# Attention scores: three products of 64 rows a head on two halves of the array, in place of two of 128 rows

## The chip, the core and the metric

One Trainium2 chip, of which one core runs the program. The metric is the device time of one execution in microseconds; the median of three runs of the kernel before is 1757.9 us (1756.42 to 1758.44).

The engines are named as the profile names them: PE is TensorE's matrix products, PEld its loads of stationary operands (weights), DVE is VectorE, ACT ScalarE, POOL GpSimd, SP the queue that issues DMAs. "f32" in a matmul row stands for float32 and for its rounded form fp32r alike.

## What is computed

Two layers: a Mamba-2 mixer, then stick-breaking attention over 16 heads of 64 features and 1024 positions. The change is in the scores of the second layer, cut here to what matters:

```
def stick_breaking_mixer(h, k, v, norm_g, w_in, q_g, w_out):
    ...
    q = rmsnorm(qg[..., :SB_WIDTH].reshape(bsz, s, SB_HEADS, SB_HEAD_DIM), q_g)
    q = (q * (1.0 / math.sqrt(SB_HEAD_DIM))).transpose(0, 2, 1, 3)
    for blk in range(s // SB_BLOCK):
        ...
        z = jnp.einsum('bhtd,bhsd->bhts', q[:, :, q0:kend], k[:, :, :kend]).astype(jnp.float32)
        ...
        log_keep = jnp.where(strict, jax.nn.log_sigmoid(-z), 0.0)
        suffix = lax.cumsum(log_keep, axis=3, reverse=True) - log_keep
        weights = jnp.where(strict, jnp.exp(jax.nn.log_sigmoid(z) + suffix), 0.0)
        outs.append(jnp.einsum('bhts,bhsd->bhtd', weights.astype(v.dtype), v[:, :, :kend]))
```

A float32 product is made of three products of rounded parts: with q = q_hi + q_lo and k = k_hi + k_lo it is q_hi k_hi + q_hi k_lo + q_lo k_hi.

## The kernel before

The first half of the span is the Mamba layer, and after it come an embedding stage, the attention (from about 924 us to 1531 us) and the output layers. Only the attention is touched.

The attention goes through eight pairs of heads (`hp`), and in each pair through four blocks of 256 positions (`p` = 3, 2, 1, 0), so 32 steps (`i`). For a block, `project` multiplies the activations with the pair's weights (L911, 24 products of 384 columns for 128 positions), `norm` scales keys and queries, and `flip` turns them with two transposes each (L1054) so that the 128 partitions hold the 64 features of head 0 and the 64 of head 1. `flip` then splits them into rounded and rest parts, and `scores` makes the products. Positions run backwards, so the scores of block `b` of 128 queries cover (8 - b) x 128 keys, in one part up to 512 columns and in two equal parts above. A pair of heads has, for each head, twelve such parts: widths 512 (three), 448 (two), 384 (three), 320 (two), 256 and 128.

How the parts lie before: `kst` holds for each head, in one column of 128 partitions, k_hi on the head's own 64 partitions and k_lo on the other 64. `qh` holds q_hi twice, on both halves, and `ql` holds q_lo on the own half and zeros on the other (zeroed once, L882). So one product over 128 rows with `qh` gives q_hi k_hi + q_hi k_lo (L1111), and one with `ql` gives q_lo k_hi (L1112). To lay this out, `flip` issues per step two ACT instructions for k_hi (L1064), four for q_hi (L1076), two DVE instructions for k_lo (L1067) and two for q_lo (L1081), each on 64 partitions.

After the scores, ACT takes the sigmoid (`s_sig`, L1119), which frees the PSUM tile `z`. DVE runs the product along the keys (`scan`, L1124), PE transposes the result (L1150, L1152), ACT and DVE split it into parts (L1158, L1163), and PE multiplies it with the values (L1171) in the accumulator `oq`.

The order of PE, ACT and DVE in the attention is made ahead of time by `Plan.order`: every step is an `op_` with an engine, an estimated duration, a rank, the ops that it comes after, and buffers (`slot`) that it takes and gives from rings of fixed size. At each point the op that can start first is put out next, ranks break ties, and the table `RANK` shifts the rank of a kind of op. The ring `z` has two tiles and `tr` three; `qh` has one.

Of the kernel before, what the change touches and what calls it, by code (L numbers as in the profile page):

```python
# [18 lines left out]
P = 128  # L19
S = 1024  # L20
# [20 lines left out]
FILL = {32: 7, 33: 6}  # L41
CHUNKS = {29: (0, 1), 30: (2, 3)}

RANK = {"project": 3, "copy_kq": -13, "sums": -16, "start": -28, "newton": -2587, "nmul": -6, "v_split": -57,
        "gate": 20, "sig": 55, "gmul": -17, "w_load": 6, "w_hi": -28, "w_lo": -45, "k_hi": 10, "k_lo": -32,
        "q_hi": -853, "q_lo": -3, "scores": -1586, "s_sig": -729, "scan": 8, "turn": -2674, "a_hi": 20,
        "a_lo": 1, "o_add": -18, "o_gate": 27, "store": -4, "r_lo": -919, "o_load": 7, "o_hi": 6, "f_load": 13,
        "f_split": -10, "fill": -19, "f_add": -1544}


def split3(nc, out, pairs):
# [18 lines left out]
class Plan:  # L70
# [789 lines left out]
def attention(k, A, rawp, hT, oTd, dbg, b2, pairs):  # L860


    tc, nc = k.tc, k.nc
    ident = k.ident
    hh, hl = hT
    mm = k.mm
    with ExitStack() as ctx:
        pp = ctx.enter_context(tc.tile_pool(name="b_pair", bufs=1, reuse_waits="tile"))
        wk = ctx.enter_context(tc.tile_pool(name="b_work", bufs=2, reuse_waits="tile"))
        sm = ctx.enter_context(tc.tile_pool(name="b_small", bufs=2, reuse_waits="tile"))  # L870
        zp = ctx.enter_context(tc.tile_pool(name="b_z", bufs=2, space=PSUM, reuse_waits="tile"))
# [6 lines left out]
        nc.gpsimd.tensor_copy(keep[:, :P], k.tri)  # L878
        zrow = keep[0:1, P:3 * P].bitcast(F32)
        kst = pp.tile([P, 2, S], F32R, name="kst")  # L880
        ql = pp.tile([P, 2, 256], F32R, name="ql")
        nc.gpsimd.memset(ql.bitcast(F32), 0.0)  # L882

        oqs = op.tile([P, 512], F32, name="oq")

        plan = Plan()
        for name, bufs in (("mm", 2), ("z", 2), ("tr", 3), ("w", 3), ("pt", 5), ("kq", 2), ("vr", 3), ("qh", 1), ("sg", 1),
                           ("of", 2), ("V", 6), ("vs", 1), ("raw", 3)):
# [11 lines left out]
        n = len(steps)  # L900
# [145 lines left out]
        def flip(i, hp, p):  # L1046
            tsl = slice(p * 256, (p + 1) * 256)
            t = {}

            def turn_(m):  # L1050
                def go():
                    t[m] = trp.tile([P, 512], F32, name="tr")[:, :256]
                    for j in range(2):
                        nc.tensor.transpose(t[m][:, j * P:(j + 1) * P], sts[hp]["kq", p][:, j, m], ident)  # L1054
                return go
            old = list(zs.get(i - 1, ()))
            ks, qs = slot("tr", 2), slot("tr", 2)
# [3 lines left out]
            qh_s = slot("qh", 2 * sum(len(parts(b)) for b in (2 * p + 1, 2 * p)))  # L1061

            def key_hi(h):
                return lambda: nc.scalar.activation(kst[own[h], h, tsl], t[0][own[h]], AF.Copy, scale=g[own[h]])  # L1064

            def key_lo(h):
                return lambda: nc.vector.scalar_tensor_tensor(  # L1067
                    kst[own[1 - h], h, tsl], t[0][own[h]], g[own[h]], kst[own[h], h, tsl].bitcast(F32),
                    op0=ALU.mult, op1=ALU.subtract)

            def query_hi(h):
                def go():
                    if h == 0:
                        tiles["qh", i] = wk.tile([P, 2, 256], F32R, name="qh", bufs=1)
                    for x in (own[h], own[1 - h]):
                        nc.scalar.copy(tiles["qh", i][x, h], t[1][own[h]])  # L1076
                return go

            def query_lo(h):
                o = own[h]  # L1080
                return lambda: nc.vector.tensor_tensor(ql[o, h], t[1][o], tiles["qh", i][o, h].bitcast(F32), op=ALU.subtract)  # L1081
            prev, pd = [], []
            for h in range(2):
                prev = [op_("k_hi", "ACT", 0.47, 10 * i + 2, key_hi(h), [fk] + prev + (old if p == 3 else []))]
                khi[i, h] = prev[0]
                pd = [op_("k_lo", "DVE", 0.49, 10 * i + 2, key_lo(h), [khi[i, h]] + pd, (), (ks,))]
                klo[i, h] = pd[0]
            for h in range(2):
                prev = [op_("q_hi", "ACT", 0.73, 10 * i + 2, query_hi(h), [fq] + prev, (qh_s,) if h == 0 else ())]
                pd = [op_("q_lo", "DVE", 0.43, 10 * i + 2, query_lo(h), prev + pd + old, (), (qs,))]  # L1090
                qlo[i, h] = pd[0]
# [6 lines left out]
        def scores(i, hp, h, b, qh_s):  # L1098
            N = (NT - b) * P
            qs = slice((b % 2) * P, (b % 2) * P + P)  # L1100
            pt_s[i, h, b] = slot("pt")
            key = ("a", hp, h, b)
            last = []
            sg = []
            for m, (ko, w) in enumerate(parts(b)):
                z_s = slot("z")

                def mul(ko=ko, w=w, m=m):
                    z = tiles["z", i, h, b, m] = zp.tile([P, 512], F32, name="z")
                    rk = kst[:, h, b * P + ko:b * P + ko + w]  # L1110
                    nc.tensor.matmul(z[:, :w], lhsT=tiles["qh", i][:, h, qs], rhs=rk, start=True, stop=False)  # L1111
                    nc.tensor.matmul(z[:, :w], lhsT=ql[:, h, qs], rhs=rk, start=False, stop=True)  # L1112
                z = op_("scores", "PE", 2 * (0.013 + w * 0.000419), 10 * i + 3, mul, [klo[i, h], qlo[i, h]] + last[:1], (z_s,), (qh_s,))
                zs.setdefault(i, []).append(z)

                def sig(ko=ko, w=w, m=m):
                    if m == 0:
                        tiles[key] = wk.tile([P, S], F32, name="pt", bufs=5)
                    nc.scalar.activation(tiles[key][:, ko:ko + w], tiles["z", i, h, b, m][:, :w], AF.Sigmoid, scale=-1.0)  # L1119
                s = op_("s_sig", "ACT", 0.19 + w * 0.00078, 10 * i + 3, sig, [z] + sg, (pt_s[i, h, b],) if m == 0 else (), (z_s,))  # L1120

                def scan(ko=ko, w=w):
                    pt = tiles[key]
                    nc.vector.tensor_tensor_scan(pt[:, ko:ko + w], pt[:, ko:ko + w], keep[:, ko:ko + w],  # L1124
                                                 pt[:, ko - 1:ko] if ko else 1.0, op0=ALU.mult, op1=ALU.max)
                sg = [s]
                last = [z, op_("scan", "DVE", 0.15 + w * 0.00208, 10 * i + 3, scan, [s] + last[1:])]
            scans[i, h, b] = last[1]

        def combine(i, hp, p):  # L1130
            lo = 2 * p
# [207 lines left out]
        for hp in range(8):  # L1339
            pair = [(4 * hp + 3 - p, p) for p in (3, 2, 1, 0)]  # L1340
            for i, p in pair:
                copies = project(i, hp, 2 * p + 1)
                if p == 1:
                    gate(i, hp, 1)
                if p == 1:
                    gate(i, hp, 0)
                copies += project(i, hp, 2 * p)
                norm(i, hp, p, (copies[0], copies[2]))
                values(i, hp, p, (copies[1], copies[3]))
            if hp + 1 < 8:  # L1350
                for q in range(4):
                    weights(hp + 1, q)
            if hp == 6:
                begun.append(op_("begin", "SPW", 0.0, 0, lambda: b2.begin(pairs), proj[6, 0][-1:]))
            for i, p in pair:
                qh_s = flip(i, hp, p)
                for h in range(2):
                    for b in (2 * p + 1, 2 * p):
                        scores(i, hp, h, b, qh_s)
                combine(i, hp, p)  # L1360
        for kk in range(KT):
            s_out(kk)
# [247 lines left out]
```

## Time and profile before

| | us |
|---|---|
| median of three runs | 1757.9 |
| the profiled execution, its own time | 1758.81 |
| span of that execution, first to last instruction | 1757.1 |
| PE busy | 1703.1 (97%) |
| PEld busy | 1450.7 (83%) |
| DVE busy | 1196.1 (68%) |
| ACT busy | 895.9 (51%) |

A matmul's record lasts longer than the time after which the next one starts, because matmuls are pipelined; what one costs on PE is read from the distance between two starts. A "busy" PE is therefore not PE at its peak. The form "128*64" of a matmul means 128 rows and 64 columns of the array; a product on 64 columns at partition 0 and one on 64 columns at partition 64 lie on different halves. In the Mamba layer L485 makes such products, alternating between the two halves, while all other products of that stretch use 128 rows and 128 columns.

### The profile page before, as it was taken

Reading aid. Unit: us, or ns where it says so; the run is one execution under the profiler, and the core shown is the slowest. Engines: PE = TensorE matmul, PEld = TensorE weight load, DVE = VectorE, ACT = ScalarE, POOL = GpSimd, SP = SyncE. Lnnn points to the kernel's source line nnn. Section 1 sums busy time; section 2 is a strip of 40 time slices with the busy share of each in tenths; the row PEclk is TensorE's granted clock in tenths of the full one; section 3 lists DMA queues with packets and bytes.
Section 4 is the critical chain, followed back from the end, with each engine's and each line's share of the span. In section 5 each row is a group of like instructions: output and inputs, shape, how many; then the busy total and the mean of one; then the engine's idle time right before and its main releaser. Section 6 shows DMA issues by size and latency. Waiting matters only on the chain.

```text
span 1757.1 us, 25573 instructions
## 1 busy us (share of the span) xinstructions
PE 1703.1 (97%) x9170; PEld 1450.7 (83%) x9170; DVE 1196.1 (68%) x2460; ACT 895.9 (51%) x1976; POOL 434.2 (25%) x452
## 2 busy tenths in 40 slices
PE   7999999999999999999999999999999999899999
PEld 6777877887887777888888999989999998778887
DVE  7678179259448846443567699999999999993232
ACT  6558339447635624222355556666575666652121
POOL 0134624524444322220001111121121214211010
PEclk9999999999999999999999999999999999899999
DMA  4222213213212365332221111111110112252100
GB/s 162 69 67 91 96 49 108 90 54 96 91 66 79 126 215 179 113 132 87 82 100 31 56 32 59 41 33 56 31 59 28 48 43 67 76 165 78 57 28 36
DMA packets 96399, 139.43 MB, mean 79 GB/s; under 512 B 18160, under 2 KB 66640, under 8 KB 96272
## 3 DMA queue, kind: packets, MB, share of 16 engines
q1 hardware_dynamic: 96272, 137.80, 24.4%
q8 instruction: 72, 1.18, 0.3%
q14 instruction: 55, 0.45, 0.1%
HBM read 108.77 MB, written 24.77 MB: 76 GB/s over the span
## 4 chain that ended last, share of the span: by engine, by line
PE 79%; DVE 13%; ACT 4%; DMA 2%; issue 2%; POOL 0%; SPq 0%; DVEq 0%; ACTq 0%
PE mm L54 38%; PE mm L911 17%; PE mm L1441 4%; PE oq L1171 3%; DVE pt L1124 3%; PE pq L54 3%; DVE v L310 2%; PE intra L485 2%; PE z L1111 2%; PE z L1112 2%; PE tr L1150 1%; PE tr L740 1%; DVE wl L1163 1%; PE inter L480 1%; PE tr L1152 1%
## 5 line engine op out<-in xcount | busy, mean ns | idle before, releaser
L54 PE MATMUL mm<-ul,wh 128*128 128x512 f32 (+1 forms) x648 | 254.0, 392 | 0.0
L54 PE MATMUL mm<-uh,wh 128*128 128x512 f32 (+1 forms) x648 | 252.4, 390 | 0.1
L54 PE MATMUL mm<-uh,wl 128*128 128x512 f32 (+1 forms) x648 | 252.4, 390 | 0.0
L1124 DVE TENSOR_TENSOR_SCAN pt<-pt,keep 128x320 f32<-128x320 f32 (+3 forms) x192 | 196.1, 1048 | 3.5 <-ACT pt L1119 1.4
L911 PE MATMUL mm<-g0h,hh 128*128 128x384 f32 x512 | 174.7, 341 | 3.6 <-ACT vr L952 1.8
L911 PE MATMUL mm<-g0l,hh 128*128 128x384 f32 x512 | 175.9, 343 | 0.0
L911 PE MATMUL mm<-g0h,hl 128*128 128x384 f32 x512 | 174.2, 340 | 0.0
L310 DVE SCALAR_TENSOR_TENSOR v<-u,convh,v 128x512 f32<-128x512 f32 x144 | 129.5, 904 | 55.1 <-ACT v L308 52.6
L997 POOL TENSOR_TENSOR vs<-vs,vr 128x256 f32<-128x256 f32 x32 | 30.5, 953 | 477.4 <-DMA vs<-vr 241.1
L54 PEld LDWEIGHTS mm<-ul,wh 128*128 128x128 f32 x648 | 121.7, 188 | 26.4 <-issue 2.3
L54 PEld LDWEIGHTS mm<-uh,wl 128*128 128x128 f32 x648 | 121.8, 188 | 25.5 <-issue 1.9
L54 PEld LDWEIGHTS mm<-uh,wh 128*128 128x128 f32 x648 | 121.7, 188 | 25.5 <-issue 1.1
L182 POOL TENSOR_TENSOR wl<-raw,wh 128x1024 fp32r<-128x1024 f32 x39 | 95.1, 2440 | 156.1 <-ACT wh L180 156.0
L1158 ACT CAST wh<-tr 128x512 fp32r<-128x512 f32 (+1 forms) x160 | 84.4, 547 | 64.2 <-PE tr L1152 59.1
L650 DVE SCALAR_TENSOR_TENSOR acc<-mm,rg,acc 128x512 f32<-128x512 f32 x64 | 47.8, 749 | 84.8 <-PE mm L54 83.2
L1119 ACT ACTIVATE pt<-z 128x320 f32<-128x320 f32 (+3 forms) x192 | 87.0, 492 | 36.4 <-PE z L1112 24.3
L1163 DVE TENSOR_TENSOR wl<-tr,wh 128x512 fp32r<-128x512 f32 (+1 forms) x160 | 96.6, 629 | 7.5 <-ACT wh L1158 6.1
L911 PEld LDWEIGHTS mm<-g0h,hh 128*128 128x128 f32 x512 | 96.5, 188 | 5.8 <-DVE GT L979 2.9
L911 PEld LDWEIGHTS mm<-g0h,hl 128*128 128x128 f32 x512 | 96.6, 189 | 0.9
L911 PEld LDWEIGHTS mm<-g0l,hh 128*128 128x128 f32 x512 | 96.5, 188 | 0.6
L723 DVE SCALAR_TENSOR_TENSOR pth<-pth,pq 128x512 f32<-128x512 f32 (+1 forms) x33 | 22.2, 672 | 108.2 <-PE pq L54 103.6
L447 ACT ACTIVATE ex<-ex,acum 128x128 f32<-128x128 f32 x256 | 86.5, 389 | 0.8
(378 smaller groups left out, 4316.6 us busy)
## 6 DMA issues: line engine op xcount, KB each, us to landing
raw<-in_w_in SPq DMA_DIRECT2D x40, 512.0 KB
ex<-acd SPq DMA_DIRECT2D x64, 256.0 KB
raw<-in_w_b SPq DMA_DIRECT2D x32, 512.0 KB
raw<-in_m_out SPq DMA_DIRECT2D x16, 512.0 KB
raw<-in_gate SPq DMA_DIRECT2D x16, 512.0 KB
graw<-gT SPq DMA_DIRECT2D x30, 256.0 KB
gT<-zs SPq DMA_DIRECT2D x28, 256.0 KB
acc<-in_x SPq DMA_DIRECT2D x8, 512.0 KB
```

What stands on the lines that cost most here:

```text
L54: nc.tensor.matmul(out, lhsT=a, rhs=b, start=(i == 0), stop=(i == n - 1))
L182: (eng or nc.gpsimd).tensor_tensor(lo, raw, hi.bitcast(F32), op=ALU.subtract)
L310: nc.vector.scalar_tensor_tensor(vv, u[:, 3 - j:3 - j + 512], w(j), vv, op0=ALU.mult, op1=ALU.add)
L447: nc.scalar.activation(x, x, AF.Relu, bias=acum[:, c:c + 1])
L650: nc.vector.scalar_tensor_tensor(acc[:, sl], ps, k.rg[:, g, t:t + 1], acc[:, sl], op0=ALU.mult, op1=ALU.add)
L911: nc.tensor.matmul(out, lhsT=a, rhs=b, start=(i == 0), stop=(i == len(prs) - 1))
L1119: nc.scalar.activation(tiles[key][:, ko:ko + w], tiles["z", i, h, b, m][:, :w], AF.Sigmoid, scale=-1.0)
L1124: nc.vector.tensor_tensor_scan(pt[:, ko:ko + w], pt[:, ko:ko + w], keep[:, ko:ko + w], pt[:, ko - 1:ko] if ko else 1.0, op0=ALU.mult, op1= ...
L1158: nc.scalar.copy(wh[:, :c], tiles["tq", key][:, :c])
L1163: nc.vector.tensor_tensor(wl[:, :c], tiles["tq", key][:, :c], wh[:, :c].bitcast(F32), op=ALU.subtract)
L1171: nc.tensor.matmul(out[:, :w], lhsT=sts[hp]["V"][j // 2][:, j % 2, h * P:(h + 1) * P], rhs=rhs, start=(j0 == lo and m == 0), stop=(j0 == N ...
L1441: nc.tensor.matmul(pss[n], lhsT=a, rhs=b, start=(q == 0 and i == 0), stop=(q == 1 and i == 11))
```

## The change

`kst` now holds k_hi of both heads in its first half and k_lo of both heads in its second, each on the head's own 64 partitions; `qh` holds q_hi and q_lo in the same way, in two buffers where there was one. `ql` and its zeros are gone. `flip` issues one instruction per step for each of k_hi, k_lo, q_hi and q_lo, on 128 partitions. A score op makes both heads at once: three products of 64 rows for each, head 0 on rows 0 to 63 of the array and head 1 on rows 64 to 127, in alternation, into two `z` tiles that it takes together. Three products are still accumulated for each score. `RANK` has new numbers, and with them the order of PE, ACT and DVE in the attention is another; of that table two lines stand here.

```diff
-RANK = {"project": 3, "copy_kq": -13, "sums": -16, "start": -28, "newton": -2587, "nmul": -6, "v_split": -57,
+RANK = {"project": 6, "copy_kq": 33, "copy_v": -1481, "square": 9, "sums": 6, "start": 11, "nmul": -17,
...
-        ql = pp.tile([P, 2, 256], F32R, name="ql")
-        nc.gpsimd.memset(ql.bitcast(F32), 0.0)
...
-            ks, qs = slot("tr", 2), slot("tr", 2)
+            ks, qs = slot("tr"), slot("tr")
...
-            def key_hi(h):
-                return lambda: nc.scalar.activation(kst[own[h], h, tsl], t[0][own[h]], AF.Copy, scale=g[own[h]])
...
-                    for x in (own[h], own[1 - h]):
-                        nc.scalar.copy(tiles["qh", i][x, h], t[1][own[h]])
...
+            def key_hi():
+                nc.scalar.activation(kst[:, 0, tsl], t[0], AF.Copy, scale=g)
+
+            def key_lo():
+                nc.vector.scalar_tensor_tensor(
+                    kst[:, 1, tsl], t[0], g, kst[:, 0, tsl].bitcast(F32), op0=ALU.mult, op1=ALU.subtract)
+
+            def query_hi():
+                tiles["qh", i] = wk.tile([P, 2, 256], F32R, name="qh", bufs=2)
+                nc.scalar.copy(tiles["qh", i][:, 0], t[1])
+
+            def query_lo():
+                q = tiles["qh", i]
+                nc.vector.tensor_tensor(q[:, 1], t[1], q[:, 0].bitcast(F32), op=ALU.subtract)
...
-                z_s = slot("z")
+                z_s = [slot("z") for _ in range(2)]
...
-                    z = tiles["z", i, h, b, m] = zp.tile([P, 512], F32, name="z")
-                    rk = kst[:, h, b * P + ko:b * P + ko + w]
-                    nc.tensor.matmul(z[:, :w], lhsT=tiles["qh", i][:, h, qs], rhs=rk, start=True, stop=False)
-                    nc.tensor.matmul(z[:, :w], lhsT=ql[:, h, qs], rhs=rk, start=False, stop=True)
...
+                    zz = [zp.tile([P, 512], F32, name="z") for _ in range(2)]
+                    ks = slice(b * P + ko, b * P + ko + w)
+                    q = tiles["qh", i]
+                    for n, (x, y) in enumerate(((0, 0), (0, 1), (1, 0))):
+                        for h in range(2):
+                            tiles["z", i, h, b, m] = zz[h]
+                            o = own[h]
+                            nc.tensor.matmul(zz[h][:, :w], lhsT=q[o, x, qs], rhs=kst[o, y, ks], start=(n == 0), stop=(n == 2))
```

PE's order in the attention, around the scores of one part of 320 columns, before. A row gives line, operation, output tile, operands and size; `z` is a score tile, `mm` the tile of a projection, and the numbers tell tiles of one name apart.

```order
L911 MATMUL mm_9886<-g0h_9773,hl1_6973 128x384
L1111 MATMUL z_9927<-kst_8291,qh_9873 128x320
L1112 MATMUL z_9927<-kst_8291,ql_8292 128x320
L1111 MATMUL z_9931<-kst_8291,qh_9873 128x320
L1112 MATMUL z_9931<-kst_8291,ql_8292 128x320
L911 MATMUL mm_9886<-g0h_9787,hh1_6971 128x384
```

The same engine with the change, around one part of 384 columns between products of the gate projection.

```order
L909 MATMUL mm_9546<-hl0_6972,g0h_8851 128x512
L909 MATMUL mm_9546<-hh0_6970,g0l_8852 128x512
L1103 MATMUL z_9568<-kst_8291,qh_9549 128x384
L1103 MATMUL z_9569<-kst_8291,qh_9549 128x384
L1103 MATMUL z_9568<-kst_8291,qh_9549 128x384
L1103 MATMUL z_9569<-kst_8291,qh_9549 128x384
L1103 MATMUL z_9568<-kst_8291,qh_9549 128x384
L1103 MATMUL z_9569<-kst_8291,qh_9549 128x384
L909 MATMUL mm_9546<-hh0_6970,g0h_8875 128x512
```

Two products a head became three, in alternation between the two heads' tiles. There are 96 such score ops; in PE's new order they make 94 stretches, since only two pairs of ops stand next to each other, and between all others stand products of 128 rows.

ACT's order where score tiles are read, before: L1119 reads a `z`, L1158 rounds turned weights.

```order
L1158 CAST wh_9233<-tr_9209 128x512
L1119 ACTIVATE pt_9238<-z_9159 128x512
L1119 ACTIVATE pt_9238<-z_9167 128x512
L1158 CAST wh_9252<-tr_9222 128x512
L1119 ACTIVATE pt_9260<-z_9249 128x448
```

With the change, where the tiles of two score ops are read: L1113 reads a `z`, the lines 948 to 1014 serve the projection, L1153 rounds turned weights.

```order
L1113 ACTIVATE pt_9252<-z_9275 128x512
L1113 ACTIVATE pt_9264<-z_9276 128x512
L1113 ACTIVATE pt_9314<-z_9304 128x128
L948 COPY kq_9234<-mm_9225 128x256
L950 COPY vr_9235<-mm_9225 128x128
L1014 ACTIVATE sg_9328<-kq_9234 128x512
L948 COPY kq_9362<-mm_9316 128x256
L950 COPY vr_9363<-mm_9316 128x128
L1153 CAST wh_9383<-tr_9374 128x384
L1153 CAST wh_9393<-tr_9378 128x512
L1153 CAST wh_9399<-tr_9386 128x512
L1113 ACTIVATE pt_9417<-z_9305 128x128
```

Before, each tile was taken and given back alone. Now a score op needs both, and its second tile can be read several instructions after its first.

## Rows read from the trace of the kernel before

**Rows 1.** The page: the chain of work that ended last, by engine.

```profile
PE 79%; DVE 13%; ACT 4%; DMA 2%; issue 2%; POOL 0%; SPq 0%; DVEq 0%; ACTq 0%
```

**Rows 2.** Busy time (and instructions) of each engine in the attention stretch.

```profile
core 0: us, PE busy (x) PEld busy (x) DVE busy (x) ACT busy (x) POOL busy (x), PEclk, DMA share, GB/s
924.00:1531.00 607.00, 590.02 (x3604) 553.03 (x3603) 542.28 (x1188) 375.86 (x905) 124.14 (x170) 0.99 0.15 46
```

**Rows 3.** Whom PE waited for in that stretch: total, times, longest.

```profile
PE tr L1150 <- DVE wl L1163: 3.6, 4, 2.2
PE tr L1054 <- DVE kq L1043: 3.0, 1, 3.0
```

**Rows 4.** PE in order of time, scores of 448 and 512: start, duration, what.

```profile
1229.48 0.34 PE L911 MATMUL mm<-g0h,hl 128*128 128x384 f32 x1
1229.66 0.36 PE L1111 MATMUL z<-kst,qh 128*128 128x448 f32 x1
...
1230.48 0.34 PE L911 MATMUL mm<-g0h,hh 128*128 128x384 f32 x1
...
1231.19 0.39 PE L1111 MATMUL z<-kst,qh 128*128 128x512 f32 x1
...
1232.11 0.34 PE L911 MATMUL mm<-g0l,hh 128*128 128x384 f32 x1
```

**Rows 5.** The same view, scores of 320 and 384 columns.

```profile
1214.43 0.31 PE L1111 MATMUL z<-kst,qh 128*128 128x320 f32 x1
...
1215.01 0.33 PE L911 MATMUL mm<-g0h,hh 128*128 128x384 f32 x1
...
1215.71 0.34 PE L1111 MATMUL z<-kst,qh 128*128 128x384 f32 x1
...
1216.40 0.34 PE L911 MATMUL mm<-g0l,hh 128*128 128x384 f32 x1
```

**Rows 6.** PE in order of time, Mamba layer, around products of L485.

```profile
298.77 1.05 PE L480 MATMUL inter<-BC,st 128*128 128x128 f32 x8
...
299.89 0.40 PE L54 MATMUL mm<-uh,wl 128*128 128x512 f32 x1
300.22 0.66 PE L485 MATMUL intra<-ex,xdt 128*64 128x128 f32 x8
300.80 0.50 PE L54 MATMUL mm<-uh,wh 128*128 128x512 f32 x1
301.24 0.66 PE L485 MATMUL intra<-ex,xdt 128*64 128x128 f32 x8
301.82 0.50 PE L54 MATMUL mm<-ul,wh 128*128 128x512 f32 x1
302.16 0.40 PE L54 MATMUL mm<-uh,wl 128*128 128x512 f32 x1
302.40 0.40 PE L54 MATMUL mm<-uh,wh 128*128 128x512 f32 x1
```

**Rows 7.** PE's weight loads there; in brackets the idle time before.

```profile
300.21 0.42 PEld L485 LDWEIGHTS intra<-ex,xdt 128*64 128x64 f32 x8 [0.36 <-PE inter L480]
300.80 0.19 PEld L54 LDWEIGHTS mm<-uh,wh 128*128 128x128 f32 x1 [0.17 <-issue]
...
302.17 0.19 PEld L54 LDWEIGHTS mm<-uh,wh 128*128 128x128 f32 x1
```

**Rows 8.** Groups by line and form, 924 to 1531 us: busy, mean ns, idle before.

```profile
L1076 ACT CAST qh<-tr 64x256 fp32r<-64x256 f32 x128 | 47.0, 367 | 2.5
L1067 DVE SCALAR_TENSOR_TENSOR kst<-tr,gkq,kst 64x256 fp32r<-64x256 f32 x64 | 30.9, 484 | 13.6 <-ACT kst L1064 12.0
L1064 ACT ACTIVATE kst<-tr,gkq 64x256 fp32r<-64x256 f32 x64 | 29.9, 468 | 6.4 <-PE tr L1054 5.9
L1081 DVE TENSOR_TENSOR ql<-tr,qh 64x256 fp32r<-64x256 f32 x64 | 26.9, 420 | 4.6 <-ACT qh L1076 2.7 <-issue 0.6
L1119 ACT ACTIVATE pt<-z 128x384 f32<-128x384 f32 x48 | 22.7, 490 | 11.4 <-PE z L1112 10.9
```

More of the change, by code (lines that the diff above doesn't have):

```diff
@@ L42 @@
 CHUNKS = {29: (0, 1), 30: (2, 3)}
-RANK = {"project": 3, "copy_kq": -13, "sums": -16, "start": -28, "newton": -2587, "nmul": -6, "v_split": -57,
[L45 to L48, printed above, removed]
+RANK = {"project": 6, "copy_kq": 33, "copy_v": -1481, "square": 9, "sums": 6, "start": 11, "nmul": -17,
+        "v_load": 6, "v_split": -17, "gate": 7, "sig": 39, "gmul": -2293, "w_load": -6, "w_hi": 6, "w_lo": -4,
+        "k_hi": -2554, "k_lo": 10, "q_hi": -24, "q_lo": 11, "scores": -737, "s_sig": 15, "scan": 24,
+        "turn": -1659, "a_hi": 26, "a_lo": -13, "prod": -35, "o_copy": -5, "o_add": 1, "o_gate": 21,
+        "r_hi": 33, "r_lo": 48, "o_hi": 56, "o_lo": -2299, "f_load": -36, "fill": -12, "f_add": -12}
 def split3(nc, out, pairs):
@@ L880, in attention @@
         kst = pp.tile([P, 2, S], F32R, name="kst")
[L881 to L882 removed]
         oqs = op.tile([P, 512], F32, name="oq")
         plan = Plan()
[L887 removed]
+        for name, bufs in (("mm", 2), ("z", 2), ("tr", 3), ("w", 3), ("pt", 5), ("kq", 2), ("vr", 3), ("qh", 2), ("sg", 1),
                            ("of", 2), ("V", 6), ("vs", 1), ("raw", 3)):
@@ L1060, in flip @@
             g = k.gkq
-            qh_s = slot("qh", 2 * sum(len(parts(b)) for b in (2 * p + 1, 2 * p)))
-            def key_hi(h):
-                return lambda: nc.scalar.activation(kst[own[h], h, tsl], t[0][own[h]], AF.Copy, scale=g[own[h]])
[L1066 to L1074, printed above, removed]
-                    for x in (own[h], own[1 - h]):
-                        nc.scalar.copy(tiles["qh", i][x, h], t[1][own[h]])
-                return go
@@ L1079, in query_lo @@
[L1079 to L1091, printed above, removed]
+            qh_s = slot("qh", sum(len(parts(b)) for b in (2 * p + 1, 2 * p)))
+            def key_hi():
[3 more added lines that the diff above has]
+                    kst[:, 1, tsl], t[0], g, kst[:, 0, tsl].bitcast(F32), op0=ALU.mult, op1=ALU.subtract)
@@ new lines, in query_hi @@
+            def query_hi():
[4 more added lines that the diff above has]
+                nc.vector.tensor_tensor(q[:, 1], t[1], q[:, 0].bitcast(F32), op=ALU.subtract)
+            x = op_("k_hi", "ACT", 0.45, 10 * i + 2, key_hi, [fk] + (old if p == 3 else []))
+            klo[i] = op_("k_lo", "DVE", 0.49, 10 * i + 2, key_lo, [x], (), (ks,))
@@ L1092, in flip @@
+            x = op_("q_hi", "ACT", 0.42, 10 * i + 2, query_hi, [fq], (qh_s,))
+            qlo[i] = op_("q_lo", "DVE", 0.43, 10 * i + 2, query_lo, [x], (), (qs,))
             return qh_s
@@ L1096, in parts, with scores @@
             return [(0, N)] if N <= 512 else [(0, N // 2), (N // 2, N // 2)]
-        def scores(i, hp, h, b, qh_s):
+        def scores(i, hp, b, qh_s):
             N = (NT - b) * P
             qs = slice((b % 2) * P, (b % 2) * P + P)
[L1101 to L1104, printed above, removed]
+            last, sg = [], [[], []]
+            for h in range(2):
+                pt_s[i, h, b] = slot("pt")
             for m, (ko, w) in enumerate(parts(b)):
-                z_s = slot("z")
+                z_s = [slot("z") for _ in range(2)]
@@ L1114, in scores @@
-                zs.setdefault(i, []).append(z)
[L1116 to L1125, printed above, removed]
@@ L1126, in scores @@
-                sg = [s]
-                last = [z, op_("scan", "DVE", 0.15 + w * 0.00208, 10 * i + 3, scan, [s] + last[1:])]
-            scans[i, h, b] = last[1]
+                    zz = [zp.tile([P, 512], F32, name="z") for _ in range(2)]
+                    ks = slice(b * P + ko, b * P + ko + w)
+                    q = tiles["qh", i]
+                    for n, (x, y) in enumerate(((0, 0), (0, 1), (1, 0))):
+                        for h in range(2):
+                            tiles["z", i, h, b, m] = zz[h]
+                            o = own[h]
+                            nc.tensor.matmul(zz[h][:, :w], lhsT=q[o, x, qs], rhs=kst[o, y, ks], start=(n == 0), stop=(n == 2))
@@ new lines, in scores, with sig, scan @@
+                z = op_("scores", "PE", 3 * (0.013 + w * 0.000419), 10 * i + 3, mul, [klo[i], qlo[i]] + last[:1],
+                        z_s, (qh_s,))
+                zs.setdefault(i, []).append(z)
+                sc = last[1:]
+                last = [z]
+                for h in range(2):
+                    def sig(ko=ko, w=w, m=m, h=h):
+                        if m == 0:
+                            tiles["a", hp, h, b] = wk.tile([P, S], F32, name="pt", bufs=5)
+                        nc.scalar.activation(tiles["a", hp, h, b][:, ko:ko + w], tiles["z", i, h, b, m][:, :w], AF.Sigmoid, scale=-1.0)
+                    s = op_("s_sig", "ACT", 0.19 + w * 0.00078, 10 * i + 3, sig, [z] + sg[h], (pt_s[i, h, b],) if m == 0 else (), (z_s[h],))
+                    sg[h] = [s]
+                    def scan(ko=ko, w=w, h=h):
+                        pt = tiles["a", hp, h, b]
+                        nc.vector.tensor_tensor_scan(pt[:, ko:ko + w], pt[:, ko:ko + w], keep[:, ko:ko + w],
+                                                     pt[:, ko - 1:ko] if ko else 1.0, op0=ALU.mult, op1=ALU.max)
+                    x = op_("scan", "DVE", 0.15 + w * 0.00208, 10 * i + 3, scan, [s] + sc[h:h + 1])
+                    last.append(x)
+                    scans[i, h, b] = x
@@ L1356, in attention @@
                 qh_s = flip(i, hp, p)
-                for h in range(2):
-                    for b in (2 * p + 1, 2 * p):
-                        scores(i, hp, h, b, qh_s)
+                for b in (2 * p + 1, 2 * p):
+                    scores(i, hp, b, qh_s)
                 combine(i, hp, p)
```

1 line of the change is left out of this document (removed).

## The prediction, made before the changed kernel was run

> **What bounds the kernel now.** I read the chain of work that ended last first: PE carries 79% of it and DVE 13% [rows 1]. Then I read the attention stretch alone, since nothing outside it changes. PE is busy 590.0 of 607 us there, DVE 542.3 and ACT 375.9 [rows 2]. So PE is full to within 17.0 us, DVE to within 65 us, and ACT has 231 us to spare. The list of waits shows how little PE stands still for others: its two largest entries are 3.6 and 3.0 us in total, both on DVE [rows 3]. A step that makes PE's work longer therefore shows in the time almost whole, and one that only relieves ACT or DVE shows little.
>
> Since a busy PE is not PE at its peak, I take the cost of a product from the distance between two starts. Four score products of 512 columns stand 1231.19 to 1232.11, so 0.23 each; 448 columns take 0.205, 320 take 0.145 and 384 take 0.173 [rows 4, 5]. It matters below that the change of kind costs nothing now: the projection product before the scores starts 0.18 before them, what a product of 384 columns takes anyway [rows 4].
>
> **What the change takes from PE.** For one part of a pair of heads PE makes four products of the part's width now. If the halves of the array run side by side, three widths remain, so each part saves one product. A pair of heads has the widths 512 (3), 448 (2), 384 (3), 320 (2), 256 and 128. In rows' numbers that is 3 x 0.23 + 2 x 0.205 + 3 x 0.173 + 2 x 0.145 = 1.91 us; 256 columns in proportion 0.12 and 128 at most 0.11, the distance of narrow products in [rows 6]. That makes 2.14 us, and over eight pairs **17.1 us**; all score products together take four times that, 68.4 us.
>
> Do halves run side by side at all? No product of the trace uses half the rows, so I take the nearest thing: L485, on halves of the columns. Eight of these last 0.66 us, one lasting 0.27, so they start 0.056 apart on the mean. Eight products of L480, the same 128 columns wide on the whole array, last 1.05, so start 0.11 apart [rows 6]. The alternating halves thus run in pairs. I assume the same of row halves.
>
> **What the change adds to PE.** The same rows price the way in and out. Products of L54 follow each other at 0.24 (302.16 to 302.40).
> - In: the L54 product at 299.89 is followed by L485 at 300.22, 0.33 later: 0.09 too many. The weight load does not run ahead: PEld stands idle 0.36 us before it and starts when the product does [rows 7].
> - The first pair is late by its exposed load: 0.66 - 0.27 - 3 x 0.11 leaves 0.06, for weights of 64 columns.
> - Out: from 300.22 to 300.80 are 0.58, of which four pairs take 0.44 and the late load 0.06; 0.08 is left. PEld again waits, 0.17, and starts with the product [rows 7].
> - After it: from 301.82 to 302.16 are 0.34, 0.10 over 0.24, the exposed load of 128 columns. The next load at 302.17 is hidden again.
>
> The second visit agrees: 300.80 to 301.24 is 0.44, one product with a late load and a way in. A visit costs 0.09 + 0.06 + 0.08 + 0.10 = 0.33 us. The scores' weights have 128 columns, not 64, so the load on the way in costs 0.10, and a visit 0.37. PE's new order has 94 visits, so **34.8 us**. Nothing covers it, because the stall is PE's own. The bounds of a visit are zero, as at today's boundaries [rows 4], and 0.37. It cannot be a gain, since those boundaries already cost nothing. I take 0.37, since [rows 6] is a switch to parts of the array and [rows 4] is none.
>
> The Trainium skill, "TensorEngine Tiling (Array Packing)", section "Key Properties", says that a change of tiling mode drains TensorE, while a change of tile within a mode does not. For column halves the trace agrees (0.09 in, 0.08 out), and for row halves no run here shows it.
>
> **What goes from ACT and DVE.** Per step four of six ACT instructions and two of four DVE instructions go. On ACT, 32 x 0.468 + 96 x 0.367 = 50 us; on DVE, 32 x 0.484 + 32 x 0.420 = 29 us [rows 8], if 128 partitions take as long as 64. Both lie beside PE's work, so I count nothing directly. They and PE's own lateness should shorten the waits: of the 17.0 us that PE idles I take a quarter, **4 us**, between none and 10. The shorter way through flip (one head's parts no longer queue behind the other's) matters only where PE waits for it; no such wait is among PE's longest [rows 3]. The zeroing of `ql` on POOL happened once before the stretch, and the freed `ql` and second `qh` only loosen things.
>
> **What else is moved.** The new ranks move weight loads on SP, the values' preparation on POOL, and the order of the three planned engines. POOL is busy 124 of 607 us and the DMA engines 15% [rows 2], so these have room. I take 0 and keep 6 us either way.
>
> A score op now takes both `z` tiles, so it waits for both sigmoids of the op before, 2 x 0.49 us [rows 8] and a hand-over. In 80 of 93 gaps PE has more than ten products to make meanwhile, over 1.1 us at 0.11 each. In 13 it has ten or fewer. A wait there also holds up the projection behind it, because PE goes in order. I take nothing for it, and up to 1 us each for the upper bound.
>
> **The sum.** -17.1 + 34.8 - 4 = +13.7 us. The profiled execution took 1758.8 and would take 1772.5; the median of the runs is 0.9 lower, so I forecast **1772** on the median's footing, 0.8% slower.
>
> **The rivals.**
> - *Row halves need no switch.* Loads for half the rows slip under the running product as loads do today. Then -17.1 stands alone, and fewer waits give at most some us: 1736 to 1743, **1741**. For it: today's loads all hide. Against it: the loads of column halves do not [rows 7]. This is the case on the other side. It decides by the price of a visit, which breaks even at 17.1 / 94 = 0.18 us. Chance 0.18.
> - *The drain is paid and the loads are hidden.* A visit costs 0.09 + 0.08 = 0.17, times 94 = 16: **1757**. Against it: both loads are late in [rows 6, 7]. Chance 0.08. The Trainium skill, "TensorE: Matmul & The Clock Gate", section "Part 2: What happens when you issue a matmul", lets a load run ahead if it goes to the background weights; the trace shows that within one mode only.
> - *The change does not do what it says:* the two heads' products run one after the other. Six products of full width against four add 34.2, and the visits 34.8: about **1823**, chance 0.05. If only the loads take turns, each part lasts at least 6 x 0.11 = 0.66 us. A pair of heads then takes 3 x 0.70 + 9 x 0.66 = 8.04 us against 8.55, so 4 us are saved instead of 17.1: **1785**, chance 0.07.
> - *The pair of `z` tiles becomes a wait.* The 13 short gaps cost about 1 us each on top: **1785**. For it: ACT's new order reads some second tiles late. Against it: ACT has 231 us free. Chance 0.08.
>
> **How the numbers follow.** My own case has 0.54, its own range 1763 to 1781 (the 6 us of order, and 0 to 10 for the waits). The range 1741 to 1788 holds it, the half-priced visit, turns of the loads, the `z` wait and about half of the case without a switch; outside are 0.05 above, some 0.09 below and a little of each tail. A measurement tells about 0.2%, 3.5 us, from no change. Faster by more: 0.18 and 0.03 of the half-priced case, 0.21. Within it: 0.06. Slower: 0.73.
>
> **What would show it.** In the profile after, the two products of a pair should start some 0.01 us apart, and three pairs of 512 columns should take about 0.7 us plus 0.10 for the first load. PEld should stand idle before the first score load and before the first load after the scores. A projection product should start over 0.3 us before the scores, and the attention stretch should be about 14 us longer. ACT's and DVE's busy time there should fall by about 50 and 29 us without helping. I am wrong if loads of half the rows start while the projection's product runs (then 1741), if the products of a pair start a product's length apart (then 1823), or if PE's list of waits gets a large entry from the sigmoids' line to the scores'.

## The result, and the profile after

The changed kernel takes 1774.8 us (median of four runs, 1774.5 to 1775.7) against 1758.2 for the kernel before, measured beside it (four runs, 1756.4 to 1758.7). The ratio is 1.0097, with a 95% interval of 1.0080 to 1.0115: 16.6 us slower. The forecast was 1772, 13.7 us slower on its own footing. The profiled execution took 1775.7 us with a span of 1774.0.

The page after, its span and each engine's busy time, share and instructions:

```profile
span 1774.0 us, 25671 instructions
...
PE 1718.0 (97%) x9362; PEld 1430.9 (81%) x9362; DVE 1166.3 (66%) x2396; ACT 843.7 (48%) x1848; POOL 431.6 (24%) x451
```

The page's chain of work breaks off early in this run, so [rows 1] has no counterpart. Where the time came from is read from the first product of the layer behind the attention. By the view of its line, before and then after (minimum, median and maximum of the durations, first and last start), it starts 17 us later:

```profile
L1441 PE MATMUL mm<-hh,oh x84: 390/396/396, 1583.0 to 1722.8; 128*128 128x512 f32 x84
L1435 PE MATMUL mm<-hh,oh x84: 390/395/397, 1599.9 to 1739.8; 128*128 128x512 f32 x84
```

The last of these 84 products starts at 1722.8 before and 1739.8 after, so from there on nothing differs. All the time is lost in the attention. Busy time of each engine there, with instructions, and then the granted clock, the DMA share and GB/s, as in [rows 2] but over a stretch 17 us longer:

```profile
924.00:1548.00 624.00, 604.97 (x3798) 532.50 (x3797) 519.01 (x1126) 326.20 (x781) 118.58 (x169) 0.98 0.15 48
```

PE is busy 15 us longer and idle 19.0 us instead of 17.0, while ACT and DVE are busy 50 and 23 us less in the longer stretch. PE still sets the end, and it is PE that got slower. PE in order of time, around the scores of one part of 384 columns; the counterpart of [rows 4, 5], and of [rows 6] for row halves:

```profile
1217.59 0.34 PE L909 MATMUL mm<-g0l,hh 128*128 128x384 f32 x1
1217.76 0.34 PE L909 MATMUL mm<-g0h,hl 128*128 128x384 f32 x1
1218.03 0.79 PE L1103 MATMUL z<-kst,qh 64*128 64x384 f32 x6
1218.74 0.44 PE L909 MATMUL mm<-g0h,hh 128*128 128x384 f32 x1
1219.02 0.34 PE L909 MATMUL mm<-g0l,hh 128*128 128x384 f32 x1
1219.20 0.33 PE L909 MATMUL mm<-g0h,hl 128*128 128x384 f32 x1
```

Every term of a visit can be read here. Projection products of 384 columns follow each other at 0.17. The last before the scores starts 0.27 ahead of them: **0.10 on the way in**. Six products fill 0.71 until the projection goes on; in turn they would need 6 x 0.173 = 1.04, as three pairs 0.52. So they run side by side, and **0.19** is left: the first pair's exposed load and the way out. The first product after takes 0.28: **0.11 for its exposed load**. PE's weight loads at the same place (brackets: idle time before), as in [rows 7]:

```profile
1217.59 0.19 PEld L909 LDWEIGHTS mm<-g0h,hl 128*128 128x128 f32 x1
1218.03 0.47 PEld L1103 LDWEIGHTS z<-kst,qh 64*128 64x128 f32 x6 [0.25 <-ACT qh L1070]
1218.74 0.19 PEld L909 LDWEIGHTS mm<-g0h,hh 128*128 128x128 f32 x1 [0.25 <-issue]
1218.85 0.19 PEld L909 LDWEIGHTS mm<-g0l,hh 128*128 128x128 f32 x1
```

PEld idles 0.25 us before both changes of kind and loads only when the product itself starts; the load after (1218.85) runs ahead again. The profile puts the first wait down to ACT's `qh`, but a change of kind in the middle of a score op, where no split part is awaited, costs as much (experiment 1). Over the 92 visits that consist of one part, the medians of the start distances are 0.094 in, 0.105 for the first load, 0.094 out and 0.106 for the load after, **0.40 us a visit** (the mean, without visits that touch a wait or the lower clock, is 0.38). The two products of a pair start 2 to 4 ns apart in 226 of 288 pairs.

The Trainium skill, "TensorEngine Tiling (Array Packing)", section "Key Properties", says that a change of tiling mode drains TensorE and that different tiles load and multiply in parallel. The trace agrees with both for row halves: 0.094 us each way, and pairs 2 to 4 ns apart.

The groups that answer to [rows 8] (busy us, mean ns, idle before and what ended it):

```profile
L1065 DVE SCALAR_TENSOR_TENSOR kst<-tr,gkq,kst 128x256 fp32r<-128x256 f32 x32 | 15.4, 480 | 6.1 <-ACT kst L1062 5.5
L1062 ACT ACTIVATE kst<-tr,gkq 128x256 fp32r<-128x256 f32 x32 | 15.3, 479 | 11.0 <-PE tr L1052 6.7 <-PE z L1103 4.0
...
L1074 DVE TENSOR_TENSOR qh<-tr,qh 128x256 fp32r<-128x256 f32 x32 | 13.3, 415 | 1.1 <-ACT qh L1070 0.9
L1070 ACT CAST qh<-tr 128x256 fp32r<-128x256 f32 x32 | 11.9, 371 | 3.3 <-PE tr L1052 3.2
```

With 128 partitions an instruction lasts what it did with 64 (371 ns against 367, 480 against 484). So ACT saves 49.7 us and DVE 29.1. PE's largest waits (total, times, longest), the counterpart of [rows 3]:

```profile
PE tr L1145 <- DVE pt L1119: 7.7, 2, 4.5
PE tr L1145 <- DVE wl L1158: 4.3, 1, 4.3
PE z L1103 <- ACT pt L1113: 4.0, 3, 2.5
```

They are fewer and longer than before, and they have moved to the end. The third is the wait for the joint pair of `z` tiles. Busy time, granted clock, DMA share and GB/s up to 1400 us and from there to the next layer, two rows for the kernel before and two for after:

```profile
924.00:1400.00 476.00, 469.17 (x2872) 441.84 (x2871) 418.92 (x947) 291.77 (x711) 84.24 (x129) 1.00 0.14 44
1400.00:1583.00 183.00, 168.51 (x978) 150.35 (x977) 169.70 (x331) 113.12 (x251) 46.34 (x46) 0.96 0.27 86
924.00:1400.00 476.00, 474.99 (x3008) 421.30 (x3007) 392.41 (x877) 252.07 (x613) 77.07 (x130) 1.00 0.13 41
1400.00:1600.00 200.00, 178.28 (x1032) 151.27 (x1031) 166.29 (x332) 100.65 (x224) 48.23 (x43) 0.93 0.26 83
```

Up to 1400 us PE's idle time falls from 6.8 to 1.0 us; behind it, it grows from 14.5 to 21.7, and the granted clock is lower there (0.93 against 0.96).

### The profile page after: what moved, and what is told of

It reads as the page before. It is cut to its first block, busy times and chain, and to the rows that moved or that the text cites. A ratio compares the mean times of both kernels' runs of the same rounds, so it can differ in the third digit from the quotient of the medians.

```text
span 1774.0 us, 25671 instructions
## 1 busy us (share of the span) xinstructions
PE 1718.0 (97%) x9362; PEld 1430.9 (81%) x9362; DVE 1166.3 (66%) x2396; ACT 843.7 (48%) x1848; POOL 431.6 (24%) x451
## 5 line engine op out<-in xcount | busy, mean ns | idle before, releaser
L1119 DVE TENSOR_TENSOR_SCAN pt<-pt,keep 128x384 f32<-128x384 f32 (+4 forms) x192 | 186.6, 1020 | 3.5 <-ACT pt L1113 3.4
L54 PEld LDWEIGHTS mm<-uh,wl 128*128 128x128 f32 x648 | 121.8, 188 | 25.7 <-issue 1.9
L1113 ACT ACTIVATE pt<-z 128x384 f32<-128x384 f32 (+4 forms) x192 | 89.9, 492 | 84.5 <-PE z L1103 68.5
L1158 DVE TENSOR_TENSOR wl<-tr,wh 128x512 fp32r<-128x512 f32 (+1 forms) x160 | 98.1, 632 | 34.4 <-ACT wh L1153 32.9
L1153 ACT CAST wh<-tr 128x512 fp32r<-128x512 f32 (+1 forms) x160 | 83.2, 546 | 66.3 <-PE tr L1147 43.2
```

The costliest lines, as they stand in the source:

```text
L54: nc.tensor.matmul(out, lhsT=a, rhs=b, start=(i == 0), stop=(i == n - 1))
L1113: nc.scalar.activation(tiles["a", hp, h, b][:, ko:ko + w], tiles["z", i, h, b, m][:, :w], AF.Sigmoid, scale=-1.0)
L1153: nc.scalar.copy(wh[:, :c], tiles["tq", key][:, :c])
L1158: nc.vector.tensor_tensor(wl[:, :c], tiles["tq", key][:, :c], wh[:, :c].bitcast(F32), op=ALU.subtract)
```

## The experiments

**The theory.** Each visit to the halves costs PE about 0.40 us that nothing covers: 94 x 0.40 = 37.5 us, against 17.1 saved, so +20.4; waits give some of it back. **The rivals:** the halves do not really run side by side; the loss is in the order of instructions (the new rank table, or the planner's estimates) and not in the switch; or the relief of ACT and DVE matters more than the forecast said.

All ratios are against the kernel before on the same chip, and "over after" is against 1774.8. Beside the experiments the kernel before took 0.2 to 1.3 us less than beside the kernel after, so these differences are good to about 1 us.

**1. More switches (two runs).** Both add a product of zeros (`zer` is a tile of zeros) to every score part, between its first pair and the others. In the first it has 64 rows, as a pair, and changes no kind; in the second 128 rows, so PE leaves the halves and comes back.

```diff
                             nc.tensor.matmul(zz[h][:, :w], lhsT=q[o, x, qs], ...)
+                        if n == 0:
+                            for h in range(2):
+                                nc.tensor.matmul(zz[h][:, :P], lhsT=zer[own[h]], rhs=kst[own[h], 0, ...].bitcast(F32), ...)
```
```diff
+                        if n == 0:
+                            nc.tensor.matmul(zz[0][:, :P], lhsT=zer, rhs=kst[:, 0, ...].bitcast(F32), ...)
```

> The control of the run with the extra product of 128 rows: at the same place one more pair of zero products of 64 rows by 128 columns, one on each half, so that no way in or out is added. Theory: 96 x 0.11 = 11 us, so 1785. Rival (any more product in the op delays the sigmoids and makes waits): the same as the run with the product of 128 rows, whatever that is.

> The changed kernel, and in every score op one more product of 128 rows by 128 columns with zero weights, put between the first pair of halves and the second; it adds zero to the scores of head 0. Theory (a visit to the halves of the array costs PE about 0.40 us, and PE is the bound): 96 more visits at 0.40, and the product itself at 0.11, make 96 x 0.51 = 49 us, so 1824, or up to 5 less if waits shrink. Rival (the order and the joint wait for two z tiles cost the time, and the drains lie beside waits anyway): the product alone, 96 x 0.11 = 11 us, so 1785.

Measured: the zero pair on the halves 1794.6 us (1.0207, 1.0190 to 1.0225), the zero product on the whole array 1828.3 us (1.0404, 1.0388 to 1.0419). PE in order of time with the zero pair (L1107):

```profile
1216.62 0.41 PE L1104 MATMUL z<-kst,qh 64*128 64x320 f32 x2
1216.87 0.38 PE L1107 MATMUL z<-kst,keep 64*128 64x128 f32 x4
1217.01 0.54 PE L1104 MATMUL z<-kst,qh 64*128 64x320 f32 x4
1217.48 0.45 PE L910 MATMUL mm<-g0l,hh 128*128 128x384 f32 x1
```

And with the zero product on the whole array (L1106):

```profile
1217.17 0.50 PE L1104 MATMUL z<-kst,qh 64*128 64x512 f32 x2
1217.61 0.49 PE L1106 MATMUL z<-kst,keep 128*128 128x128 f32 x2
1218.03 0.73 PE L1104 MATMUL z<-kst,qh 64*128 64x512 f32 x4
1218.69 0.45 PE L1169 MATMUL oq<-wh,V 128*128 128x256 f32 x2
```

The zero pair cost 19.8 us, not the expected 11: the zeros are plain float32, and each of the two products has two records (x4), so it takes two narrow products' time, 0.22 us a pair by the starts and 96 x 0.21 = 20 on the clock. With 0.21 for the product the theory gives the zero product on the whole array 1833, or up to 5 less; measured are 1828.3. Both kernels carry the zeros, so their difference is clean of them: 33.7 us for 96 added changes out of and into the halves, **0.35 us each** on the clock. From 1217.17 to 1218.03 are 0.86, for one pair of 512 columns (0.23) and two narrow products (0.22): 0.41 for the switch, as in a visit. PE's idle time up to the next layer is 3.8 us less than with the zero pair (17.5 against 21.3), which takes part of the 0.41 back. The price thus belongs to the change of kind, repeats with every change, and reaches the end almost whole.

**2. The same parts without halves.** Queries padded with zeros in the other head's rows, so that all six products of a part have 128 rows and PE never switches. There is one query tile instead of two, and q_hi and q_lo take two instructions each instead of one, so the planner's order may move too.

```diff
-                nc.scalar.copy(tiles["qh", i][:, 0], t[1])
+                for o, h in zip(own, range(2)):
+                    nc.scalar.copy(tiles["qh", i][o, h, 0], t[1][o])
...
-                            nc.tensor.matmul(zz[h][:, :w], lhsT=q[o, x, qs], rhs=kst[o, y, ks], ...)
+                            nc.tensor.matmul(zz[h][:, :w], lhsT=q[:, h, x, qs], rhs=kst[:, y, ks], ...)
```

> The new layout of keys, but queries padded with zeros on the other head's 64 rows, so that all six products of a part use 128 rows and the array never changes its mode; one query tile instead of two, and two instructions instead of one for q_hi and for q_lo. Theory: six widths instead of three, 51 us more, and 94 visits at 0.40 less, 37.5 us: 14 us more, so 1789, 6 us either way for the order. Rival (no price of a visit): 51 us more, 1826.

Measured: 1785.0 us (1.0158, 1.0143 to 1.0173), 10.2 over after. Twice the columns (+51.3) and no visits (-37.5) should give +13.8. PE in order of time:

```profile
1216.95 0.27 PE L1152 MATMUL tr<-ident,pt 128*128 128x128 f32 x1
1216.98 1.12 PE L1108 MATMUL z<-kst,qp 128*128 128x320 f32 x6
1217.94 0.40 PE L1171 MATMUL oq<-wh,V 128*128 128x256 f32 x2
```

From 1216.95 to 1217.94 are 0.99: a narrow product of 0.11 and six of 320 columns at 0.145, 0.87. Nothing is left for a way in or out. Twice the width costs only 10 us more than the halves.

**3. Side by side or in turn (two runs).** First the program's order: all three products of head 0, then those of head 1.

```diff
-                    for n, (x, y) in enumerate(((0, 0), (0, 1), (1, 0))):
-                        for h in range(2):
+                    for h in range(2):
+                        for n, (x, y) in enumerate(((0, 0), (0, 1), (1, 0))):
```

> The changed kernel with the three products of head 0 first and then the three of head 1; order of the ops and number of visits stay. Theory (the halves run side by side when products alternate): five or six widths instead of three, since only the last of head 0 and the first of head 1 can overlap; a width of all parts is 17.1 us, so 34 to 51 us more, 1809 to 1826. Rival (the halves share nothing in time, or PE is not the bound): no change, 1775.

Measured: 1775.2 us (1.0099, 1.0084 to 1.0114), no different from after. The edit did not do what it was made for. PE in order of time:

```profile
1217.37 0.34 PE L909 MATMUL mm<-g0h,hl 128*128 128x384 f32 x1
1217.64 0.80 PE L1103 MATMUL z<-kst,qh 64*128 64x384 f32 x6
1218.37 0.44 PE L909 MATMUL mm<-g0h,hh 128*128 128x384 f32 x1
```

Six products still take 0.73, and by their starts they come as three pairs, the two of a pair 10 ns apart, with 0.28 and 0.18 from pair to pair. Products on one half take turns (next run), so each pair holds one product of either head: head 1's first, fourth in the program, starts beside head 0's first. So this run cannot tell the two cases apart. A second run can: both heads' products on rows 0 to 63. Head 1's scores are then made from head 0's parts, so they are other scores; the rest of the program stays.

```diff
-                            o = own[h]
+                            o = own[0]
```

> The changed kernel, with the products of both heads on rows 0 to 63 of the array: the scores of head 1 are made from head 0's parts, so the result is another, and the number of instructions, their sizes, the visits and the order stay. Theory (the halves run side by side, and PE is the bound): six widths instead of three in every part, 51 us more, less up to 6 of waits: 1820 to 1826. Rival (side by side brings little): under 1790.

Measured: 1820.4 us (1.0360, 1.0341 to 1.0379), 45.6 over after. PE in order of time:

```profile
1232.55 0.27 PE L1147 MATMUL tr<-ident,pt 128*128 128x128 f32 x1
1232.75 1.14 PE L1103 MATMUL z<-kst,qh 64*128 64x320 f32 x6
1233.82 0.50 PE L1166 MATMUL oq<-wh,V 128*128 128x256 f32 x2
```

Six products of 320 columns now fill 1.07: 6 x 0.145 = 0.87 plus 0.20 for load and way out. Side by side is worth 46 of the 51.3 us that the widths promise; PE's idle time up to the next layer is 6 us less than in after (16.5 against 22.7). The rival that the change does not do what it says falls.

**4. Fewer visits.** The blocks of 128 and 256 columns of a pair of heads share one `z` tile a head and one visit: 88 visits instead of 94. The planner's order moves with it.

```diff
-                for b in (2 * p + 1, 2 * p):
-                    scores(i, hp, b, qh_s)
+                if p == 3:
+                    scores_both(i, hp, qh_s)
+                else:
+                    for b in (2 * p + 1, 2 * p):
+                        scores(i, hp, b, qh_s)
```

> The changed kernel, with the scores of the two narrow blocks of a pair of heads (128 and 256 columns) in one op and one z tile a head, so that PE's order has 88 visits instead of 94; the planner's order moves with it. Theory: 6 x 0.40 = 2.4 us less, 1772, with some us of order either way. Rival (visits cost nothing): 1775.

Measured: 1771.8 us (1.0083, 1.0068 to 1.0098), 3.0 less than after. Six visits at 0.40 are 2.4. The intervals overlap, so alone it proves little; it has the sign and size that the theory gives. It is the fastest variant of the kernel after, and still slower than the kernel before.

**5. The order of instructions (three runs).** The rank table of before in the kernel after; the table of after in the kernel before; and the planner told that a score op takes 0.4 us longer.

```diff
-RANK = {"project": 6, "copy_kq": 33, "copy_v": -1481, ...
+RANK = {"project": 3, "copy_kq": -13, "sums": -16, ...
```
```diff
-                z = op_("scores", "PE", 3 * (0.013 + w * 0.000419), ...
+                z = op_("scores", "PE", 0.4 + 3 * (0.013 + w * 0.000419), ...
```

> The changed kernel with the table of ranks of the kernel before. Theory (visits cost, the order is worth some us): 1769 to 1781. Rival (the new order makes the kernel slower): near 1758, at most 1765.

> The kernel before with the table of ranks of the changed kernel. Theory: 1752 to 1764. Rival (the new order makes the kernel slower): 1770 or more.

> The changed kernel, with the planner told that a score op costs PE 0.40 us more. Theory (the stall is PE's own, and 93 or so visits stay): the order can only save waits, so 1770 to 1778. Rival (the loss comes from an order made for cheap scores): 1765 or less.

Measured: after with the old table 1781.5 us (1.0132, 1.0115 to 1.0149), before with the new table 1765.8 (1.0049, 1.0034 to 1.0064), and the planner with the visits 1775.9 (1.0103, 1.0088 to 1.0118). The two swaps lie 0.5 and 1.8 us above their expected ranges. Each table serves its own kernel, by 7 to 8 us, so the tables do not explain the loss; with either one shared by both kernels, after is still 9 us (new table) or 23 us (old) the slower. How much of the 16.6 us is the change's own is thus known to this range only. Telling the planner of the switch brings nothing. The swapped tables show their loss at the sigmoids of the `z` tiles (4.0 and 0.6 us with their own tables); PE's largest wait in after with the old table:

```profile
PE z L1103 <- ACT pt L1113: 12.0, 3, 7.8
```

and in before with the new one:

```profile
PE z L1111 <- ACT pt L1119: 9.6, 6, 7.8
```

**6. The relief of ACT and DVE (three runs).** The work that the change removed is put back: first in its old place, by splitting keys and queries on 64 partitions again (the queries' rounding twice), with the order left alone.

```diff
-                nc.scalar.activation(kst[:, 0, tsl], t[0], AF.Copy, scale=g)
+                for o in own:
+                    nc.scalar.activation(kst[o, 0, tsl], t[0][o], AF.Copy, scale=g[o])
...
-                nc.scalar.copy(tiles["qh", i][:, 0], t[1])
+                for o in own + own:
+                    nc.scalar.copy(tiles["qh", i][o, 0], t[1][o])
...
```

> The changed kernel, with the splitting instructions on 64 partitions as before: two for k_hi, four for q_hi (two of them repeat the work of the others), two for k_lo and two for q_lo; the order of ops stays. ACT gets back some 50 us of work and DVE some 29. Theory (their relief was worth about 4 us): 0 to 6 us more, 1775 to 1781. Rival (the relief hid a higher price of the visits): over 10 us more, 1785 or above.

Measured: 1790.7 us (1.0190, 1.0174 to 1.0205), 16 over after where the theory allowed 6. By PE's starts the loss grows evenly, about 0.5 us a step, and PE stands idle before a score product 24 times instead of 3. Then the same amount far from the scores, by repeating the rounding of the weights on ACT and every second rest on DVE:

```diff
-                        nc.scalar.activation(sts[hp]["W"][kk][0][:, sl], part(), AF.Copy, scale=g)
+                        for _ in range(2):
+                            nc.scalar.activation(sts[hp]["W"][kk][0][:, sl], part(), AF.Copy, scale=g)
...
```

> The changed kernel, with work added to ACT and DVE away from the splits: each rounding of a weight (112 of 0.50 us on ACT in the attention) is made twice, and each second rest (56 of 0.48 us on DVE) too, so 56 us more on ACT and 27 on DVE, about what the change took from them; order and splits stay. Theory (their relief as such is worth little; the run with more splits lost 16 us because the scores wait for the splits themselves): 0 to 6 us more, 1775 to 1781. Rival (the amount of work on ACT and DVE costs): 10 us or more, 1785 or above.

Measured: 1797.2 us (1.0224, 1.0207 to 1.0241), 22 over after, where the theory again allowed 6. Of PE's waits there, those for the split parts:

```profile
PE z L1103 <- DVE kst L1065: 5.1, 5, 1.5
...
PE z L1103 <- DVE qh L1074: 2.3, 1, 2.3
```

PE now waits for the split parts, which share ACT and DVE with the repeated roundings; after has no such wait among its largest. Last, the first edit again with the planner told of the longer splits:

```diff
-            x = op_("k_hi", "ACT", 0.45, ...
+            x = op_("k_hi", "ACT", 0.94, ...
...
-            x = op_("q_hi", "ACT", 0.42, ...
+            x = op_("q_hi", "ACT", 1.47, ...
...
```

> The run with the splits on 64 partitions again, but the planner is told what they last now (0.94, 0.97, 1.47 and 0.84 us instead of 0.45, 0.49, 0.42 and 0.43), so the order moves. Theory (the 16 us of the run before came from an order that counted on shorter splits; ACT and DVE have room): within 6 us of the changed kernel, 1775 to 1781. Rival (the work of ACT and DVE itself costs): 1787 or more, as with the old order.

Measured: 1820.2 us (1.0356, 1.0340 to 1.0372), 45 over after and far above the theory's range; it lies in the rival's "1787 or more", but not as with the old order. PE's largest wait up to 1500 us:

```profile
PE z L1107 <- ACT pt L1117: 17.7, 3, 6.0
```

The planner's other order lets PE stand before the joint `z` pair, so this run tests an order and not the relief.

Did the relief hide a higher price of the visits? I add up PE's start distances up to the next layer, each against the median for its kind of place in the same trace. Products and visits then cost in all three runs what they cost in after, to about 1 us. What grows are the waits, from 25.7 us in after to 37.4, 38.3 and 56.0, small late starts (2.1 to 8.0, 5.2 and 3.7), and in the last two runs the products at the lower clock (9.1 to 14.2 and 19.3). A visit is no dearer, so that rival falls. It stays open what the relief is worth in an order fitted to the longer splits. The kernel before bounds it: it has this work and its own table, and PE idles 17.0 us in all [rows 2]. Settled is that with the order of after, the work cannot come back for nothing: 16 to 22 us.

## Why the prediction was right, point by point

- **PE bounds the kernel, and what it is late shows almost whole:** held. By the medians of its start distances, widths and visits make PE 20.4 us later, and 16.6 reach the end.
- **-17.1 for three widths instead of four:** held. The pairs run side by side (2 to 4 ns apart), and products on one half cost 45.6 of 51.3 us (experiment 3).
- **+34.8 for 94 visits at 0.37:** the mechanism was right, the size a little low. A visit costs 0.40: 0.094 in (said 0.09), 0.105 for the first load (0.10), 0.094 out (0.08) and 0.106 after (0.10). By these medians that is 37.5 us, so 2.7 of the 2.9 us by which the forecast was short; by the mean visit it is 36.
- **-50 on ACT and -29 on DVE, counted as -4:** the durations held (49.7 and 29.1). The remainder, 20.4 - 16.6 = 3.8, fits the number, but that is partly luck. PE's idle time did shrink up to 1400 us, by 5.8 us, as the prediction says of a later PE; 7.2 us more behind 1400 us undid it, and over the whole attention PE idles 19.0 us, not less than the 17.0 of [rows 2]. Added up as in experiment 6, the 17 us are about 18 more for products and visits (a mean visit is 0.38 us, below the median's 0.40), 2 less for waits, 2 more at the lower clock and 1 to 2 less for small late starts. The waits count as less here, although the idle time does not, because up to the next layer there are 19 instead of 36 and each costs some 0.16 us beyond its idle time. So the remainder is in part the visit's median, and only about 2 us of it are waits. "One that only relieves ACT or DVE shows little" is not borne out in that generality: with the order of after kept, putting the work back cost 16 and 22 us.
- **0, and 6 either way, for the moved order:** a little narrow. The tables are worth 7 and 8 us to their own kernels. With one table for both kernels the change costs 9 or 23 us, so that the forecast came within 3 us is in part luck too.
- **The pair of `z` tiles:** three waits, 4.0 us, less than the 13 of the rival. The mechanism is real, though: under other orders it made waits of 12.0 and 17.7 us.
- **The rivals.** No switch (1741) falls with the idle loads and with experiments 1 and 2. The drain alone with hidden loads (1757) falls with 0.105 and 0.106 of late loads in each visit. Halves or loads in turn (1823, 1785) fall with the pairs' starts and the half that took 45.6 us more.

## What to carry to other kernels

Price a use of part of TensorE's array by its visits, and not only by the columns that it saves: here a visit costs 0.40 us, more than a product of 512 columns (0.23), so a visit pays only if it saves two of these, or 0.40 us of other PE time. Take the price from any place in the same trace that already switches, even if it splits the array the other way; column halves in another layer gave 0.33, or 0.37 with the longer weight load, for the 0.40 of row halves. And room on an engine does not make its work free: here ACT is busy 52% and DVE 83% of the stretch, and in a fixed order added work still made PE wait. Before counting a relief at nothing, put the work back and look, with an order fitted to each kernel.

## What the runs showed of the hardware that was not expected

- **Products on different row halves start out of the program's order.** With three products of head 0 written ahead of three of head 1, the trace shows three pairs, the two of a pair 10 ns apart, and the same time (1775.2 against 1774.8 us). So the prediction's "PE goes in order" does not hold between the halves. The halves behave here like two queues; alternating the heads in the program brought nothing. That each keeps its own order was not looked at apart.
- **A plain float32 product leaves two records and takes two narrow products' time:** 0.21 us for 128 columns on the halves (experiment 1), where a narrow product of the rounded kind takes 0.11.
- **The granted clock fell where PE waited long.** In the kernel of the last experiment PE waits three times for about 6 us; stretches of it, busy time of the engines and then the granted clock:

```profile
924.00:1200.00 276.00, 274.42 (x1715) 243.01 (x1714) 228.45 (x521) 164.69 (x397) 34.83 (x70) 1.00 0.12 38
1200.00:1300.00 100.00, 89.41 (x541) 78.25 (x539) 74.36 (x167) 54.94 (x134) 12.58 (x25) 0.95 0.16 49
```

  It is 1.00 of the upper level (2.4 GHz) in the 276 us where PE idles 1.6, and 0.95 on the mean in the 100 us where it idles 10.6. By the sums of experiment 6, an estimate, about 10 of the 45 us go with the lower clock (19.3 against 9.1) and 30 with the waits (56.0 against 25.7).
